# Another order for a mixture of experts' products on one core, and a routing whose splits are all VectorE's

## The chip, the cores and the metric

One of the eight cores of a Trainium2 chip runs the whole program: two layers of a first block (a state space mixer, an attention that picks its keys, two MLPs) and then a block with two attentions and 32 experts. The metric is the device time of one execution in microseconds. Five engines work side by side, each through its own list of instructions in order: TensorE (PE, with its weight loads PEld), VectorE (DVE), ScalarE (ACT), GpSimd (POOL) and SyncE (SP). SyncE starts nearly all loads from the chip's memory, GpSimd the gathers and the scattered additions; all of them are carried by the same 16 DMA engines.

## The reference, cut to what matters

The change touches the last block only. 512 tokens choose 4 of 32 experts each; an expert is three products of 1024 x 1024 with biases.

```python
logits = h @ router_w + router_b
top_logit, top_e = lax.top_k(logits, 4)
top_w = softmax(top_logit)
# for each expert e and the tokens xe that chose it
gate = minimum(xe @ w_gate[e] + b_gate[e], 7.0)
up = clip(xe @ w_up[e] + b_up[e], -7.0, 7.0)
act = (up + 1) * (gate * sigmoid(1.702 * gate))
y[tokens] += top_w * (act @ w_down[e] + b_down[e])
```

Everything is in float32. The 32 experts' weights are 403 MB, and each is read once.

## The kernel before

**Ranks and sizes.** The routing counts each expert's tokens and sorts the experts: rank 0 is expert 0 by fixed choice, then the ranks go down in size. The program is written for capacities by rank. Rank 1 has two tiles of 128 tokens, ranks 2 and 3 (`HEAVY` is 1 to 3) a tile of 128 and one of 64, ranks 0 and 4 to 10 one tile of 128; these eleven are called large here, the last eight middle. Ranks 11 to 21 (`LIGHT`) have 64 tokens, ranks 22 to 31 (`TINY`) 32. What does not fit goes through a loop at the end (`overflow`).

**Products.** An expert has three units: gate (0), up (1) and down (2), each with four loads of 1 MB (`fetch`, L1429) into eight buffers (`raw`). For a large expert ScalarE rounds each half of a load to a high part `wh` (L1772), VectorE forms the low part `wl` (L1774), and three matmuls of 128x512 are made of each (high by high, high by low, low by high: L170 to L172), over two halves of the columns and eight blocks of rows: 48 matmuls a tile, and 2 for the bias (L1832), which comes from a tile that holds the biases as high and low parts (`bias`). A tile of 64 tokens holds high and low parts side by side and needs 32 and 2 (L1826, L1827). A load's buffer is free when the low part is made. There are five buffers each for `wh` and `wl`, so splits run at most two and a half loads ahead of the matmuls. For small experts (light and tiny) TensorE takes the weights as they are, in full float32 (L1804), with 2 or 4 column groups side by side; such a buffer is free when the matmuls of the load are done. After the matmuls VectorE and ScalarE form gate and up, and GpSimd adds the weighted rows of down to the output (L1890). The rows of an expert's tokens are gathered by GpSimd some units earlier (L1713) and transposed by TensorE (L1738, L1727).

**What sets the order.** `units` writes out the list of the 96 units, and `run` goes through it; every engine's list follows from that. Before, the large experts come as 0, 4, 1, 5, 2, 6, 3, 7, 8, 9, 10, and two units of small experts stand ahead of each large unit: behind a heavy expert's name in the list tiny ones are drawn, else light ones. The small units form a `lane` in which a small expert's down comes one unit after the next one's gate. A unit issues its loads as it goes, so SyncE's queue has the loads in this order, and one of them waits until a buffer of the eight is free; large units ask for their first two loads (`ahead`) while the small unit before is at work.

**Routing.** `route` runs between the last logits and the first product. It loads the biases to raw tiles, which lie in three of the five `wh` buffers (L1528), and forms their high parts (L1530) and low parts (L1533) as they come. `first` finds the tokens of expert 0, gathers its rows (`gather`, L1713) and transposes and splits them (`tiles`, L1738, L165, L166), so that its product can start before the ranks are known. The rest sorts the experts (`perm`, L1559), transposes the sums (L1570), applies the order (L1575, L1576) and counts the ranks within each expert (L1587, L1588, `place` L1597). For the first two loads of expert 0's gate, GpSimd forms the low parts in VectorE's place (L1774, the `early` case).

## Time and profile before

| | |
|---|---|
| median of three runs | 2980.98 us (2974.2 to 2983.88) |
| the profiled execution | 2984.59 us, of which the span from first to last instruction 2982.8 us |
| TensorE busy, granted clock over the span | 2677.6 us (90%), 0.946 |
| VectorE, ScalarE, GpSimd busy | 1770.5, 1191.8, 245.2 us |
| bytes over the DMA engines | 595.95 MB, 200 GB/s over the span |
| first and last matmul of the experts | 1826.3 and 2966.3 us |

Times in the rows are from the start of the span. A row of the windows view has its bounds, its length, then for each engine the busy time and, in brackets, the instructions, then the granted clock of TensorE as a share of full, the mean busy share of the 16 DMA engines (which reaches 1.02 in the records) and the rate in GB/s. A row of a timeline has start, duration from the first start to the last end of the merged instructions, engine, line, operation, output and inputs, shapes, the number of instructions (x), and in square brackets the idle time of the engine before it with what ended that. Matmuls overlap, so one that takes 0.39 us can follow another 0.23 us after it; of a small expert's full float32 matmul (L1804) the records hold two instructions.

### The profile page before, as it was taken

What the parts mean: (1) busy time and instruction counts of PE and PEld (TensorE: products, weight loads), DVE (VectorE), ACT (ScalarE), POOL (GpSimd) and SP (SyncE); (2) the same over time, 40 slices, a digit from 0 to 9 for tenths busy, and PEclk for the clock granted to TensorE, in tenths of its full rate; (3) what the DMA queues carried; (4) which work ended last, traced back from release to release, by engine and by line L of the source; (5) the groups of instructions that cost most, each with busy time, mean ns of one, the idle gap of its engine ahead of it and who ended that gap; (6) DMA issues with size and microseconds to landing.
All of it is one profiled execution on the core that took longest, in us unless ns stands there. A gap on an engine that the chain in (4) does not pass through costs nothing. (4 is left out here: it accounts for less than half of the span.)

```text
span 2982.8 us, 38289 instructions
## 1 busy us (share of the span) xinstructions
PE 2677.6 (90%) x14182; PEld 1996.0 (67%) x14182; DVE 1770.5 (59%) x3419; ACT 1191.8 (40%) x2208; POOL 245.2 (8%) x229
## 2 busy tenths in 40 slices
PE   5599999987999999899998997999989989988986
PEld 3488777886778888788888775556455455444553
DVE  6967565578874444589777558444444444444443
ACT  5353232454863333366655434332233232333232
POOL 3000000142000000200000002110110110110010
PEclk9799999998999999999999997999989999999997
DMA  3024454321023333211122555998999998999997
GB/s 116 15 99 176 150 197 156 94 60 54 29 93 127 96 96 99 93 50 41 53 60 72 181 198 203 385 361 358 349 353 363 342 357 353 350 359 376 381 406 295
DMA packets 193999, 595.95 MB, mean 200 GB/s; under 512 B 34960, under 2 KB 106056, under 8 KB 141320
## 3 DMA queue, kind: packets, MB, share of 16 engines
q1 hardware_dynamic: 179744, 564.33, 50.8%
q0 software_dynamic: 8752, 28.58, 3.4%
q8 instruction: 113, 1.85, 0.2%
q10 hardware_dynamic: 5312, 0.54, 0.1%
q14 instruction: 78, 0.64, 0.1%
HBM read 574.49 MB, written 21.53 MB: 200 GB/s over the span
## 5 line engine op out<-in xcount | busy, mean ns | idle before, releaser
L1804 PE MATMUL lac<-raw,xtf 128*32 128x256 f32 (+1 forms) x2976 | 378.6, 461 | 6.4 <-DMA raw<-in_w_down_dram 3.8
L152 DVE TENSOR_TENSOR wl<-wr,wh 128x1024 fp32r<-128x1024 f32 (+2 forms) x222 | 262.3, 1187 | 177.6 <-ACT wh L150 173.8
L150 ACT CAST wh<-wr 128x1024 fp32r<-128x1024 f32 (+2 forms) x228 | 228.8, 1008 | 295.4 <-PE acc L172 162.0
L1774 DVE TENSOR_TENSOR wl<-raw,wh 128x1024 fp32r<-128x1024 f32 x260 | 303.7, 1219 | 36.3 <-ACT wh L1772 35.2
L171 PE MATMUL wide<-wl,xth 128*128 128x512 f32 x576 | 259.8, 451 | 30.8 <-DVE wl L1774 30.6
L170 PE MATMUL wide<-wh,xth 128*128 128x512 f32 x576 | 256.1, 446 | 33.7 <-ACT wh L1772 32.4
L1772 ACT CAST wh<-raw 128x1024 fp32r<-128x1024 f32 x264 | 260.8, 1045 | 62.5 <-PE wide L172 37.0
L1804 PEld LDWEIGHTS lac<-raw,xtf 128*32 128x32 f32 (+1 forms) x2976 | 126.3, 119 | 193.8 <-issue 155.2
L170 PE MATMUL mm<-wh,xh 128*128 128x384 f32 (+2 forms) x664 | 230.1, 346 | 27.0 <-ACT gate L1264 12.8
L172 PE MATMUL wide<-wh,xtl 128*128 128x512 f32 x576 | 250.2, 434 | 0.0
L171 PE MATMUL mm<-wl,xh 128*128 128x384 f32 (+2 forms) x664 | 222.7, 335 | 3.1 <-DVE wl L152 2.9
L172 PE MATMUL mm<-wh,xl 128*128 128x384 f32 (+2 forms) x664 | 222.5, 335 | 1.2 <-DVE xl L166 1.2
L171 PE MATMUL acc<-wl,ffh 128*128 128x512 f32 x512 | 199.3, 389 | 0.7 <-DVE wl L152 0.7
L172 PE MATMUL acc<-wh,ffl 128*128 128x512 f32 x512 | 199.4, 390 | 0.0
L170 PE MATMUL acc<-wh,ffh 128*128 128x512 f32 x512 | 198.6, 390 | 0.0
L171 PEld LDWEIGHTS wide<-wl,xth 128*128 128x128 f32 x576 | 122.2, 212 | 99.4 <-DVE wl L1774 56.2
L170 PEld LDWEIGHTS wide<-wh,xth 128*128 128x128 f32 x576 | 121.3, 211 | 88.9 <-ACT wh L1772 46.6
L170 PEld LDWEIGHTS mm<-wh,xh 128*128 128x128 f32 x664 | 129.0, 194 | 44.1 <-ACT gate L1264 17.1
L172 PEld LDWEIGHTS wide<-wh,xtl 128*128 128x128 f32 x576 | 122.2, 212 | 34.7 <-issue 11.4
L171 PEld LDWEIGHTS mm<-wl,xh 128*128 128x128 f32 x664 | 129.0, 194 | 9.8 <-DVE wl L152 5.3
L172 PEld LDWEIGHTS mm<-wh,xl 128*128 128x128 f32 x664 | 129.2, 195 | 7.0 <-DVE xl L166 1.9
L1890 POOL DMA_INDIRECT out_dram<-xy,si x35 | 65.4, 1867 | 662.1 <-DVE xy L1889 482.2
(641 smaller groups left out, 5417.7 us busy)
## 6 DMA issues: line engine op xcount, KB each, us to landing
raw<-in_w_gate_dram SPq DMA_DIRECT2D x128, 1024.0 KB, 8.5
raw<-in_w_up_dram SPq DMA_DIRECT2D x128, 1024.0 KB, 11.4
raw<-in_w_down_dram SPq DMA_DIRECT2D x128, 1024.0 KB, 7.3
wr<-in_mlp_w_dram SPq DMA_DIRECT2D x128, 512.0 KB, 3.7
adaraw<-in_w_ada_dram SPq DMA_DIRECT2D x12, 2048.0 KB, 7.5
wr<-in_w_in_dram SPq DMA_DIRECT2D x16, 512.0 KB, 3.9
wr<-in_att_w_out_dram SPq DMA_DIRECT2D x12, 512.0 KB, 3.9
wr<-in_w_in_dram SPq DMA_DIRECT2D x48, 128.0 KB, 2.4
```

What stands on the lines that cost most here:

```text
L150: nc.scalar.copy(hi, raw)
L152: (eng or nc.vector).tensor_tensor(lo, raw, hi.bitcast(F32), op=OP.subtract)
L170: mmul(ps, ah, bh, start=first, stop=False)
L171: mmul(ps, ah, bl, start=False, stop=False)
L172: mmul(ps, al, bh, start=False, stop=last)
L1772: S.copy(wh, raw[:, j])
L1774: (G_ if early and t == 0 and c < 2 else V).tensor_tensor(wl, raw[:, j], wh.bitcast(F32), op=OP.subtract)
L1804: T.matmul(ps[m * g:m * g + m], x, raw[:, j, N * g:N * g + N], start=False, stop=c == 3 and j == 1)
L1890: G_.indirect_dma_start(out=out_rows, out_offset=bass.IndirectOffsetOnAxis(ap=si[:rows], axis=0), in_=y, in_offset=None, bounds_check=511, ...
```

## The change

Three things are altered. In `units`, the table `many` names for every large expert how many units of small experts follow each of its three units: 1 for ranks 0, 4, 6, 7 and 9, 2 for ranks 5, 8 and 10, 4 for rank 1, 3 for ranks 2 and 3; behind heavy experts these are tiny ones, behind the others light ones. The sequence of large experts and the `lane` stay. In `expert`, VectorE forms all low parts. In `route`, only the loads of the raw biases stay at the head; their high and low parts are formed at the end of the function, and so is expert 0's transposed tile, which `first` had made.

```diff
 def units():
-    small = []
-    for r in big[1:]:
-        for _ in range(2):
-            n = next(tiny) if r in HEAVY else next(light, None)
-            small.append(next(tiny) if n is None else n)
+    light, tiny = iter(LIGHT), iter(TINY)
+    many = [(0, 1), (4, 1), (1, 4), (5, 2), (2, 3), (6, 1), (3, 3), (7, 1), (8, 2), (9, 1), (10, 2)]
+    small = [next(tiny if r in HEAVY else light) for r, n in many for _ in range(n)]
     lane = [(small[0], 0), (small[0], 1)]
     for p, r in zip(small, small[1:]):
         lane += [(r, 0), (p, 2), (r, 1)]
...
-    order = [(0, 0), (0, 1), next(lane), (0, 2)]
-    for u in [(r, t) for r in big[1:] for t in range(3)]:
-        order += [next(lane), next(lane), u]
-    return order + list(lane)
+    lane = iter(lane + [(small[-1], 2)])
+    order = []
+    for r, n in many:
+        for t in range(3):
+            order += [(r, t)] + [next(lane) for _ in range(n)]
+    order[1:3] = order[2:0:-1]
+    return order
@@ route
+        raws = []
         for n in ("b_gate_2", "b_up_2", "b_down_2"):
-            raw = self.wp.tile([P, D], F32, name="bw", tag="wh")[:, :512]
+            raws.append(self.wp.tile([P, D], F32, name="bw", tag="wh")[:, :512])
             for i in range(4):
...
-            x = bp.tile([P, 512], F32R, name=n)
-            S.copy(x, raw)
-            for i in (1, 3):
-                s = slice(NE * i, NE * i + NE)
-                V.tensor_tensor(x[s], raw[s], x[s].bitcast(F32), op=OP.subtract)
-            self.bias.append(x)
@@ route, at its end
         V.tensor_copy(self.cnt, o)
+        self.xt0 = self.tiles(self.x0)
+        for n, raw in zip(("b_gate_2", "b_up_2", "b_down_2"), raws):
+            x = bp.tile([P, 512], F32R, name=n)
+            S.copy(x, raw)
...
@@ first
-        x0 = self.gather(gi)
+        self.x0 = self.gather(gi)
...
-        self.xt0 = self.tiles(x0)
@@ expert
-                    (G_ if early and t == 0 and c < 2 else V).tensor_tensor(wl, raw[:, j], wh.bitcast(F32), op=OP.subtract)
+                    V.tensor_tensor(wl, raw[:, j], wh.bitcast(F32), op=OP.subtract)
```

The engines' lists are not in the order of the code alone; a scheduler lays them out. VectorE's list in the routing, before, from the operands of expert 0's gather (`gi`) to the third block's sums (`sw` is the sums, `sv` what comes of expert 0's table):

```order
L1641 TENSOR_SCALAR gi_16459<-tr 128x1
L1550 TENSOR_TENSOR one<-one,w_16423 128x128
L1649 CAST ax_16441<-w_16464 128x4
L1550 TENSOR_TENSOR one<-one,w_16423 128x128
L1650 TENSOR_TENSOR ax_16441<-w_16464,ax_16441 128x4
L1551 TENSOR_REDUCE sw<-one 128x32
L1533 TENSOR_TENSOR b_up_16410<-bw,b_up_16410 32x512 x2
L1666 COPY sv_16474<-tr 128x4
L1551 TENSOR_REDUCE sw<-one 128x32
```

and after:

```order
L1543 SCALAR_TENSOR_TENSOR kc<-mm,c_keyc 128x1
L1769 TENSOR_TENSOR wl<-raw,wh 128x1024
L1637 TENSOR_SCALAR gi_16447<-tr 128x1
L1644 TENSOR_REDUCE w_16452<-w_16451 128x4
L1538 TENSOR_TENSOR one<-one,w_16411 128x128
L1645 CAST ax_16429<-w_16452 128x4
L1538 TENSOR_TENSOR one<-one,w_16411 128x128
L1646 TENSOR_TENSOR ax_16429<-w_16452,ax_16429 128x4
L1539 TENSOR_REDUCE sw<-one 128x32 x2
L1661 COPY sv_16462<-tr 128x4
```

The two subtractions of b_up's low part stand between the sums before and have left; one split (`wl<-raw`) now stands ahead of `gi`.

TensorE's list in the routing, before, from expert 0's two tables to the counts of the ranks (`xy` is expert 0's gathered tile, `sw` the sums):

```order
L1639 MATMUL tr<-ax_16441,oh 128x4 x4
L1653 MATMUL tr<-ax_16441,oh 128x4 x4
L1738 MATMUL tr<-c_ident,xy 128x128 x8
L1570 MATMUL tr<-c_ident,sw 64x128 x4
L1575 MATMUL out<-two,rxt 128x64 x4
L1576 MATMUL out<-perm,c_tokp_72 128x32
L1588 LDWEIGHTS before
```

and after:

```order
L1635 MATMUL tr<-ax_16429,oh 128x4 x4
L1649 MATMUL tr<-ax_16429,oh 128x4 x4
L1558 MATMUL tr<-c_ident,sw 64x128 x4
L1563 MATMUL out<-two,rxt 128x64 x4
L1564 MATMUL out<-perm,c_tokp_72 128x32
L1733 MATMUL tr<-c_ident,xy 128x128 x8
L1576 LDWEIGHTS before
```

The tile's eight transpositions stood ahead of the sums' transposition and its products; they now stand behind.

TensorE's list at a heavy expert, before, from the last matmuls of rank 1's gate product to the first of its up product (`lac` is a small expert's product, 64x512 for light and 32x256 for tiny ones):

```order
L1804 MATMUL lac<-raw,xtf 32x256 x8
L170 MATMUL wide<-wh,xth 128x512
L171 MATMUL wide<-wl,xth 128x512
L172 MATMUL wide<-wh,xtl 128x512
L1727 MATMUL tr<-c_ident,gl 128x128 x2
L1796 MATMUL lac<-b_down_16419,pick 128x256 x2
L1700 MATMUL tr<-aux,ohs 128x4 x4
L1727 MATMUL tr<-c_ident,xg 128x128 x4
L1804 MATMUL lac<-raw,xtf 32x256 x8
L1700 MATMUL tr<-aux,ohs 128x4 x4
L1796 MATMUL lac<-b_up_16410,pick 128x256 x2
L170 MATMUL wide<-wh,xth 128x512 x2
```

and after, all that stands between the two:

```order
L1799 MATMUL lac<-raw,xtf 64x512 x16
L1791 MATMUL lac<-b_up_16583,pick 128x256 x2
L1799 MATMUL lac<-raw,xtf 32x256 x16
L1791 MATMUL lac<-b_gate_16579,pick 128x256
L1799 MATMUL lac<-raw,xtf 32x256 x8
L1791 MATMUL lac<-b_gate_16579,pick 128x256
L1799 MATMUL lac<-raw,xtf 32x256 x8
L1791 MATMUL lac<-b_down_16587,pick 128x256 x2
L1722 MATMUL tr<-c_ident,gl 128x128 x2
L1695 MATMUL tr<-aux,ohs 128x4 x4
L1722 MATMUL tr<-c_ident,xg 128x128 x2
L1799 MATMUL lac<-raw,xtf 32x256 x24
```

Before, eight matmuls of a tiny down product lie between the two large ones, and the rest of the small units among the large product's; after, a whole light down product, a whole tiny up product and 24 of the 32 matmuls of a tiny gate product stand between them.

## Rows read from the trace of the kernel before

**Rows 1.** Stretch of the experts' products: length, engines' busy us, clock, DMA share, GB/s

```profile
1826.30:2966.30 1140.00, 1032.34 (x5553) 612.01 (x5553) 547.55 (x811) 358.75 (x489) 101.51 (x68) 0.93 0.93 361
```

**Rows 2.** The same view: the stage in eleven pieces, mostly between large gate products' ends

```profile
1826.30:1906.10 79.80, 79.80 (x344) 51.65 (x344) 51.72 (x91) 34.27 (x39) 7.67 (x5) 0.97 0.87 346
1906.10:2021.40 115.30, 104.32 (x567) 63.35 (x570) 54.31 (x91) 34.33 (x48) 13.82 (x9) 0.93 0.94 362
2021.40:2136.80 115.40, 108.88 (x601) 66.50 (x598) 54.38 (x80) 34.04 (x49) 10.96 (x8) 0.97 0.90 339
2136.80:2245.10 108.30, 97.90 (x534) 58.18 (x534) 48.28 (x71) 31.70 (x42) 9.21 (x6) 0.92 0.95 369
2245.10:2362.30 117.20, 105.79 (x570) 63.97 (x569) 58.83 (x88) 37.90 (x56) 10.62 (x8) 0.93 0.89 340
2362.30:2470.50 108.20, 97.26 (x534) 58.15 (x537) 47.97 (x71) 31.60 (x42) 9.51 (x6) 0.92 0.95 369
2470.50:2587.30 116.80, 105.93 (x567) 63.90 (x567) 58.11 (x87) 37.93 (x55) 9.58 (x7) 0.93 0.88 340
2587.30:2695.40 108.10, 98.75 (x395) 50.74 (x396) 49.13 (x70) 31.48 (x40) 9.17 (x6) 0.94 0.96 370
2695.40:2799.00 103.60, 94.01 (x425) 49.37 (x426) 48.76 (x71) 31.53 (x42) 9.17 (x6) 0.95 0.94 361
2799.00:2887.90 88.90, 77.61 (x546) 47.59 (x550) 44.00 (x56) 31.85 (x45) 7.60 (x4) 0.94 1.01 407
2887.90:2966.30 78.40, 62.09 (x503) 38.61 (x502) 32.06 (x38) 22.14 (x31) 4.20 (x3) 0.84 0.95 389
```

**Rows 3.** Timeline of TensorE (start us, us, engine, line, operation, tiles, shapes)

```profile
1902.74 0.39 PE L171 MATMUL wide<-wl,xth 128*128 128x512 f32 x1
1902.97 0.39 PE L172 MATMUL wide<-wh,xtl 128*128 128x512 f32 x1
...
1906.24 3.65 PE L1804 MATMUL lac<-raw,xtf 128*64 128x512 f32 x16
...
2904.39 3.72 PE L1804 MATMUL lac<-raw,xtf 128*32 128x256 f32 x64
...
2910.47 0.80 PE L170 MATMUL wide<-wh,xth 128*128 128x512 f32 x1 [1.32 <-ACT wh L1772]
...
2914.03 0.63 PE L170 MATMUL wide<-wh,xth 128*128 128x512 f32 x1
2914.46 0.63 PE L171 MATMUL wide<-wl,xth 128*128 128x512 f32 x1
```

**Rows 4.** Timeline of VectorE in the routing

```profile
1799.87 0.68 DVE L1533 TENSOR_TENSOR b_gate<-bw,b_gate 32x512 fp32r<-32x512 f32 x1
...
1804.70 8.55 DVE L1533 TENSOR_TENSOR b_up<-bw,b_up 32x512 fp32r<-32x512 f32 x2
...
1815.23 1.61 DVE L1559 TENSOR_SCALAR perm<-c_iota,kc 128x32 f32<-128x32 f32 x1
...
1820.56 1.22 DVE L1774 TENSOR_TENSOR wl<-raw,wh 128x1024 fp32r<-128x1024 f32 x1
...
1824.33 0.19 DVE L1578 TENSOR_SCALAR permf<-out 128x32 f32<-128x32 f32 x1 [2.55 <-PE out L1576]
```

**Rows 5.** Timeline of GpSimd in the routing

```profile
1804.69 1.03 POOL L1713 DMA_INDIRECT xy<-hx,gi  x1 [6.72 <-DVE sw L1551]
...
1805.75 6.94 POOL L1774 TENSOR_TENSOR wl<-raw,wh 128x1024 fp32r<-128x1024 f32 x3
...
1814.46 2.34 POOL L1774 TENSOR_TENSOR wl<-raw,wh 128x1024 fp32r<-128x1024 f32 x1 [1.77 <-ACT wh L1772]
```

**Rows 6.** Timeline of TensorE in the routing

```profile
1809.15 1.10 PE L1738 MATMUL tr<-c_ident,xy 128*128 128x128 f32 x4 [3.62 <-DMA xy<-hx,gi]
...
1820.04 1.06 PE L1570 MATMUL tr<-c_ident,sw 128*64 128x128 f32 x4 [5.41 <-DVE xtl L166]
...
1826.27 0.77 PE L170 MATMUL wide<-wh,xth 128*128 128x512 f32 x1 [0.57 <-DVE cnt L1610]
```

More of the change, by code (lines that the diff above doesn't have):

```diff
@@ L1367, in units @@
 def units():
-    mids, light, tiny = list(range(HEAVY[-1] + 1, LIGHT[0])), iter(LIGHT), iter(TINY)
-    big = [0]
-    for h in HEAVY:
-        big += [mids.pop(0), h]
-    big += mids
-    small = []
-    for r in big[1:]:
-        for _ in range(2):
-            n = next(tiny) if r in HEAVY else next(light, None)
-            small.append(next(tiny) if n is None else n)
-    small += list(light) + list(tiny)
+    light, tiny = iter(LIGHT), iter(TINY)
+    many = [(0, 1), (4, 1), (1, 4), (5, 2), (2, 3), (6, 1), (3, 3), (7, 1), (8, 2), (9, 1), (10, 2)]
+    small = [next(tiny if r in HEAVY else light) for r, n in many for _ in range(n)]
     lane = [(small[0], 0), (small[0], 1)]
@@ L1383, in units @@
         lane += [(r, 0), (p, 2), (r, 1)]
-    lane.append((small[-1], 2))
-    lane[-3:] = [lane[-2], lane[-3], lane[-1]]
-    lane = iter(lane)
-    order = [(0, 0), (0, 1), next(lane), (0, 2)]
-    for u in [(r, t) for r in big[1:] for t in range(3)]:
-        order += [next(lane), next(lane), u]
-    return order + list(lane)
+    lane = iter(lane + [(small[-1], 2)])
[5 more added lines that the diff above has]
+    return order
 class Moe:
@@ L1524, in route @@
         self.bias = []
+        raws = []
         for n in ("b_gate_2", "b_up_2", "b_down_2"):
[L1526 removed]
+            raws.append(self.wp.tile([P, D], F32, name="bw", tag="wh")[:, :512])
             for i in range(4):
[L1528 to L1534 removed]
+                nc.gpsimd.dma_start(raws[-1][NE * i:NE * i + NE], a[n][0][:, i // 2 * 512:i // 2 * 512 + 512])
         m8, one, sw, selb, onesb, iota = self.m8, self.one, self.sw0, self.selb, self.onesb, self.iota
@@ L1610, in route @@
         V.tensor_copy(self.cnt, o)
+        self.xt0 = self.tiles(self.x0)
+        for n, raw in zip(("b_gate_2", "b_up_2", "b_down_2"), raws):
+            x = bp.tile([P, 512], F32R, name=n)
+            S.copy(x, raw)
+            for i in (1, 3):
+                s = slice(NE * i, NE * i + NE)
+                V.tensor_tensor(x[s], raw[s], x[s].bitcast(F32), op=OP.subtract)
+            self.bias.append(x)
     def pools(self):
```

1 line of the change is left out of this document (removed).

## The prediction

> **What bounds the kernel now.** I read the stretches first, then the timelines of the engines where the change works. [rows 1] is the stage of the experts' products, 1140.0 us at a DMA share of 0.93 and a granted clock of 0.93; ahead of it lies the routing, in which TensorE mostly waits. In the stage neither engine is full, so the question is who waits for whom and where. [rows 2] cuts it into eleven pieces, each but the first and last between the ends of the gate products of two neighbouring large experts (nine products a piece). Let me call (1 - share) x length the DMA time that is lost. It is 10.4, 6.9, 11.5, 5.4, 12.9, 5.4, 14.0, 4.3, 6.2, 0 and 3.9 us: 80.9 in all. The three pieces of 0.88 to 0.90 are those with two products of a heavy expert (ranks 1, 2, 3); the piece of 1.01 has only tiny experts behind its large ones and loses nothing. So the transfers take 1140 - 81 = 1059 us, and for the 94 products that are still to be loaded (two are prefetched) that is 11.27 us a product. TensorE's own need: matmuls of a large product start 0.228 us apart at the full clock [rows 3], so a product of one tile (50 matmuls) needs 11.4 us, rank 1 (100) 22.8, ranks 2 and 3 (84) 19.2; a light product needs 7.3 us (twice the 3.65 of half a product), a tiny one 4.0 (3.72 and its biases) [rows 3]. A large product is thus at or above the loads' pace, a small one below it, and eight buffers of 1 MB carry a surplus of two products at most.
>
> The routing is a chain with one odd spot. VectorE's two subtractions for b_up take 8.55 us together, though one of the same on b_gate took 0.68 [rows 4]. Beside them GpSimd runs three splits from 1805.75 on, 6.94 us, until 1812.69 [rows 5]; VectorE gets free right behind that. The `perm` of the ranks takes 1.61 us beside the fourth Pool split, 1814.46 to 1816.80; `permf`, of the same size, takes 0.19 [rows 4, 5]. Everything of the ranks waits behind: the first transposition of the sums at 1820.04, the first large matmul at 1826.27 [rows 6].
>
> **The change, part by part.** *Pool's splits go to VectorE, the biases' parts behind the ranks.* The chain from 1804.70 on loses 8.55 us. It gains 1.22 (one split, the price of [rows 4]), which now stands ahead of `gi`, whose gather feeds expert 0's tile: the gather goes out at 1805.9 in place of 1804.69 [rows 5], and its transpositions, 1809.15 before [rows 6], come at 1810.4. `perm` then ends at 1816.84 - 8.55 + 1.22 - 1.4 = 1808.1. In the old program the ranks' transposition had waited 5.41 us for `xtl`, expert 0's tile, by 1820.04, because both go through the same two PSUM banks [rows 6]; the new order puts the ranks' transpositions and their products ahead of the tile's. From 1820.04 to `permf` at 1824.33 it was 4.3 us, so `permf` comes at about 1812.4, the tile's eight transpositions take 2.2 us (1.10 for four [rows 6]), the ranks' counts follow at 1814.7, `cnt` and `place` as before 1.8 us later, with half of b_down's part (0.7) in between: 1817.2 for the first large matmul, against 1826.27. The other splits wait on VectorE behind b_down, the second row block at 1819.5; the first six matmuls at half clock (0.43 us each, [rows 3]) cover that nearly. Gain 9 us. Bounds: 4 us, if three of the extra splits (3 x 1.22) and the 1.22 in the gather's path all stand in the way; 12 us, if the ranks' counts do not wait for the tile's transpositions. I take 9, since each step has its row.
>
> The Trainium skill (SBUF — State Buffer, section Who interferes with whom) says that a VectorE instruction with two SBUF inputs and a GpSimd instruction that reads SBUF exclude each other, the later one blocking until the one that holds the port is through. By the letter, one Pool split (6.94 / 3 = 2.3 us) would be the price and the gain nearer to 4 us. The trace has VectorE blocked through all three splits, so I keep 9; with 4 it would be 2966, inside the forecast's own range.
>
> What the cover was: GpSimd's splits freed the first two load buffers at 1810.4 and 1816.8; now they come free about 9 us later, at 1819.5 and 1822. These loads are expert 0's down weights, used two products later only, so it costs nothing; the buffers behind them are freed by the products themselves and move up by the 9 us. GpSimd's queue has only the next gathers behind the splits, and these wait for the ranks anyway. The overflow's small sums move behind the first product on VectorE: nothing waits for them.
>
> *The order of the experts.* No matmul, load or evacuation is added or removed; every product keeps its price. What changes is which loads stand behind which large product. The load of TensorE by a group (a large product and what follows it), against 11.27 us a product:
> before: rank 1 with two tiny 30.8 of 33.8 = 0.91; ranks 2, 3 with two tiny 27.2 = 0.80, with one light and one tiny 30.5 = 0.90, with two light 33.8 = 1.0; a middle one with two light 26.0 = 0.77; with two tiny, at the end, 19.4 = 0.57.
> after: a middle one with one light (12 groups beside expert 0's three) 18.7 of 22.5 = 0.83; with two light (9 groups) 0.77; rank 1 with four tiny 38.8 of 56.4 = 0.69; ranks 2 and 3 with three (6 groups) 31.2 of 45.1 = 0.69.
> From [rows 2] the loss of each load: the two pieces with six groups of 0.77 lose 10.5, 1.75 each or 5.2% of 33.8. The six pieces with heavy experts (9 heavy products, 9 middle ones) lose 56.1; less 9 x 1.75 leaves 40.4, 4.5 a heavy product or 13% at a load of about 0.9. At 0.57 nothing is lost. On that line 0.83 loses 9%, 2.0 us a group, and 0.69 loses 3%. After: 12 x 2.0 = 24; 9 x 1.75 = 16; heavy 3% of (3 x 56.4 + 6 x 45.1) = 14; the first piece 10 and the end 4 as before. That is 68 in place of 81: 13 us gained. Bounds: 40 gained (no loss at heavy ones and none added), and a loss of 36 (the second rival). It's a small gain by a table that looks much better balanced, because the light experts, which cost nearly twice a tiny one, now all stand behind the middle ones.
>
> Sum: 2984.6 (the profiled execution) - 9 - 13 = 2962.6. The runs' median, 2981.0, lies 3.6 lower; part of that is scatter (2974.2 to 2983.9), and I forecast 2961.
>
> **The rivals.**
> *Order neutral, 0.22.* Middle groups lose as much as heavy ones save: then only the 9 us are left, 2972 to 2976. For it: the two sums of loss above differ by a sixth only, and a piece as a whole (nine products) shows a loss that rises between 0.77 and 0.81 of load more steeply than my line.
> *One light product can't carry a middle one, slower, 0.11.* With one light behind it, a middle product has 22.5 - 18.7 = 3.8 us for everything else (transpositions, tables, waits for splits, half clock). Above that TensorE sets the pace there, while behind the heavy ones the loads set it, and eight buffers don't join the two. The piece from 2587.3 has 108.1 us for 78 us of products: 10 us per large one, if none of it is waiting for loads. Then: first six products 68, twelve groups of 28.7 = 344, nine of 36 = 324, 39 products behind and with the heavy ones at 11.27 = 440, together 1176 for 1140: +36 - 9, so 3011. Against it: the first piece, where the loads lay ready, has 79.8 us for 67.5 of products, 3.1 us per large one, just below the point. At 2910.47 a large product waits 1.32 us and then runs at 0.43 us a matmul [rows 3], half clock, 3.2 us in all over 16 matmuls.
> The Trainium skill (TensorE: Matmul & The Clock Gate, section HAM oscillation) has it that bursts between waits for transfers start throttled each time. By that, 3.2 us would come on top of the 3.1, 6.3 per large one: 2.5 us over the point in twelve groups, 30 us, and a time of 2991; of the 0.11 I put 0.03 on this form. The clock of 0.84 in the last piece [rows 2] agrees; that of 0.97 in the first, where TensorE was never starved, is why I don't charge it to middle groups.
> *Large gain, 0.13.* The heavy ones' 40 us go wholly and middle groups lose only their 5.2%: 44 us lost in place of 81, 2981 - 46 + 3 = 2938.
> *No gain in the routing, 0.07.* Expert 0's first product waits for the splits on VectorE or for its loads; the order alone gives 2968 to 2972.
>
> **How the numbers follow.** Forecast 0.47, at 2950 to 2970. A difference under 0.3% (8.9 us: below 2972.0 or above 2989.9) can't be told from none. Faster: 0.93 of the forecast, a third of the neutral case, the large gain, half of the last rival: 0.68. Slower: nearly all of the second rival, 0.11. The rest, 0.21, is the same. The range leaves out half of the slower rival above and the ends of the large gain below: 2930 to 2990.
>
> **What would show it.** Routing: no VectorE instruction of more than 1.3 us between 1800 and 1817, transpositions of the sums ahead of the tile's, the first large matmul at 1816 to 1819. Order: the pieces with heavy experts at a DMA share of 0.96 or more, the middle pieces with one light at 0.90 to 0.93, the stage some 1127 us long. Wrong, if the heavy pieces keep 0.88 to 0.90, if a middle group with one light takes more than 25 us, or if the last loads land later behind the end of TensorE's work than now.

## The result

| | median | runs |
|---|---|---|
| before | 2981.77 us | 4 (2974.2 to 2983.88) |
| changed | 2913.26 us | 4 (2912.07 to 2914.09) |

The ratio is 0.9775 [0.9759, 0.979]: 68 us faster. The forecast of 2961 and its range, 2930 to 2990, had the sign right and the size three times too small.

The profiled execution has a span of 2911.1 us (2982.8 before). Of these 71.7 us, 55.3 lie in the stage of the products. The last bias load goes out at 1792.32 in place of 1797.48, 5.2 us earlier, and it lies ahead of anything that the change touches; the profiled executions further down have it between 1787.5 and 1796.1, so that of before began its routing late, and I take these 5.2 us for scatter. The routing gives another 12, and the end behind the last matmul is 0.7 us longer than it was.

The stage in stretches, most again from the end of one large gate product to the end of another (us, length, busy time of the five engines, granted clock, DMA share, GB/s; the last row is the whole stage):

```profile
1809.20:1892.80 83.60, 81.72 (x353) 52.36 (x353) 58.76 (x99) 35.76 (x43) 7.31 (x5) 0.95 0.90 356
...
1970.50:2128.40 157.90, 139.38 (x1057) 85.73 (x1060) 63.69 (x112) 39.62 (x63) 17.72 (x13) 0.94 1.00 398
...
2237.40:2367.80 130.40, 117.00 (x809) 72.73 (x812) 61.63 (x100) 39.67 (x61) 18.13 (x10) 0.91 0.98 387
...
2438.10:2565.80 127.70, 114.54 (x807) 71.07 (x807) 60.91 (x99) 39.48 (x60) 17.20 (x9) 0.93 1.00 403
2565.80:2635.20 69.40, 64.88 (x324) 38.87 (x324) 44.35 (x64) 30.07 (x39) 8.54 (x5) 1.00 0.99 390
2635.20:2740.40 105.20, 96.02 (x387) 48.98 (x388) 47.74 (x63) 31.00 (x39) 8.23 (x5) 0.95 0.98 382
2740.40:2811.40 71.00, 67.37 (x283) 38.09 (x283) 41.85 (x50) 29.29 (x36) 6.72 (x3) 1.00 0.95 363
2811.40:2893.90 82.50, 75.66 (x311) 34.81 (x310) 33.48 (x38) 20.48 (x25) 5.43 (x3) 0.98 0.84 333
1809.20:2893.90 1084.70, 999.20 (x5553) 593.57 (x5553) 552.38 (x818) 359.98 (x494) 113.58 (x68) 0.96 0.96 382
```

Read against [rows 1, 2]: the stage went from 1140.0 to 1084.7 us, TensorE's busy time in it from 1032 to 999, the clock from 0.93 to 0.96, the transfers from 361 to 382 GB/s. The pieces with two products of a heavy expert (157.9 us with 15 products, 130.4 and 127.7 with 12) now take 10.5 to 10.9 us a product at a share of 0.98 to 1.00, where they took 12.8 to 13.0. The piece with one light product behind each of three middle ones (71.0 us for six, from 2740.40) takes 11.8; one like it, in which one of the three is tiny (69.4, from 2565.80), takes 11.6. The piece with two light ones (105.2 for nine, from 2635.20) takes 11.7, 3 us less in all than the same nine products before (108.1, from 2587.30 in [rows 2]).

The kinds of the small products need a correction. The lane puts a small expert's down product behind the next one's gate, so what stands behind a large product is shifted against what was drawn for it. Of the 30 small products behind heavy experts 24 are tiny and six light; of the twelve that stand singly behind middle ones four are tiny.

The routing, TensorE and then VectorE:

```profile
1806.24 1.98 PE L1733 MATMUL tr<-c_ident,xy 128*128 128x128 f32 x8
...
1809.16 0.77 PE L170 MATMUL wide<-wh,xth 128*128 128x512 f32 x1 [0.57 <-ACT pick L1755]
```

```profile
1802.30 0.23 DVE L1547 TENSOR_SCALAR perm<-c_iota,kc 128x32 f32<-128x32 f32 x1
...
1802.62 0.68 DVE L1605 TENSOR_TENSOR b_up<-bw,b_up 32x512 fp32r<-32x512 f32 x1
...
1806.35 0.19 DVE L1566 TENSOR_SCALAR permf<-out 128x32 f32<-128x32 f32 x1 [1.15 <-PE out L1564]
```

`perm` takes 0.23 us (1.61 in [rows 4]), a part of b_up 0.68 (8.55 for two), and the first large matmul follows the last bias load's issue by 16.8 us, where it was 28.8 (1826.27 in [rows 6] less 1797.48).

Part of this is given back. The first piece of the stage takes 83.6 us, and 79.2 with the same order and the old routing (`order_alone`, experiment 1). VectorE, and then TensorE, in the changed kernel:

```profile
1811.33 6.90 DVE L1769 TENSOR_TENSOR wl<-raw,wh 128x1024 fp32r<-128x1024 f32 x6
...
1819.81 0.69 DVE L1692 TENSOR_TENSOR ohs<-slot,place 128x512 fp32r<-128x512 f32 x1
```

```profile
1830.30 0.78 PE L1722 MATMUL tr<-c_ident,xg 128*128 128x128 f32 x4 [1.76 <-DMA xg<-hx,gi]
```

Seven splits (six of them in this row) now stand ahead of the tables of the next experts (`ohs`), which begin 10.7 us behind the first large matmul; in `order_alone` it is 0.5. The gather of the next rows goes out 14.8 us behind that matmul, 11.8 in `order_alone`, and TensorE waits 1.76 us for it. The matmuls behind that wait start 0.43 us apart at first, at half clock, where they were 0.23 apart. How much of the 4.4 us this makes was not tested.

### The profile page after: what moved, and what is told of

Same layout as the page of the kernel before. It is cut to its first block, busy times and chain, and to the rows that moved or that the text cites. A ratio compares the mean times of both kernels' runs of the same rounds, so it can differ in the third digit from the quotient of the medians.

```text
span 2911.1 us, 38304 instructions
## 1 busy us (share of the span) xinstructions
PE 2642.2 (91%) x14182; PEld 1975.6 (68%) x14182; DVE 1765.1 (61%) x3423; ACT 1191.3 (41%) x2208; POOL 248.4 (9%) x225
## 5 line engine op out<-in xcount | busy, mean ns | idle before, releaser
L171 PE MATMUL wide<-wl,xth 128*128 128x512 f32 x576 | 252.4, 438 | 30.1 <-DVE wl L1769 29.8
L170 PE MATMUL wide<-wh,xth 128*128 128x512 f32 x576 | 245.0, 427 | 18.8 <-ACT wh L1767 18.1
L172 PE MATMUL wide<-wh,xtl 128*128 128x512 f32 x576 | 239.6, 416 | 0.0
L171 PEld LDWEIGHTS wide<-wl,xth 128*128 128x128 f32 x576 | 115.8, 201 | 101.4 <-DVE wl L1769 54.5
L170 PEld LDWEIGHTS mm<-wh,xh 128*128 128x128 f32 x664 | 128.5, 194 | 43.7 <-ACT gate L1264 16.8
L1885 POOL DMA_INDIRECT out_dram<-xy,si x35 | 75.7, 2163 | 609.9 <-DVE xy L1884 407.5
```

What stands on the lines that cost most here:

```text
L170: mmul(ps, ah, bh, start=first, stop=False)
L171: mmul(ps, ah, bl, start=False, stop=False)
L172: mmul(ps, al, bh, start=False, stop=last)
L1885: G_.indirect_dma_start(out=out_rows, out_offset=bass.IndirectOffsetOnAxis(ap=si[:rows], axis=0), in_=y, in_offset=None, bounds_check=511, ...
```

## The experiments

**1. Order and routing apart.** `order_alone` is the kernel before with the new `units`; `routing_alone` the changed kernel with the old one.

```diff
 def units():
-    for u in [(r, t) for r in big[1:] for t in range(3)]:
-        order += [next(lane), next(lane), u]
+    for r, n in many:
+        for t in range(3):
+            order += [(r, t)] + [next(lane) for _ in range(n)]
```

> The kernel before with the new order of the experts only; the routing keeps GpSimd's splits and the early biases' parts. Theory A (the order is worth nearly all of it, and the routing adds to it independently): the stage of the products takes 1085 to 1092 us in place of 1140, the first large matmul stays 28 to 30 us behind the last bias load's issue (28.8 before), and the time is 2923 to 2933. Rival B (the shorter routing is what gives the stage its head start, the order alone is worth the 13 us that I forecast): a stage of 1120 to 1130 and a time of 2965 to 2972.

> The changed kernel with the old order of the experts; only the routing is changed. Theory A: the first large matmul 16 to 18 us behind the last bias load's issue (16.8 in the changed kernel, 28.8 before), the stage 1135 to 1142 as before, the time 2967 to 2973, that is 9 to 15 less. Rival B: the stage shortens as well, to 1110 or less, and the time is under 2950.

Measured: `order_alone` 2922.95 us against 2979.32 for the kernel before on the same chip, 0.9826 [0.9809, 0.9843]; `routing_alone` 2969.33, 0.9965 [0.9954, 0.9976]. So 56 and 10 us, and together they make the 66 to 68 of the change. The order alone gives its stage without any help of the routing (the first piece and the whole stage of `order_alone`):

```profile
1821.40:1900.60 79.20, 79.17 (x346) 51.46 (x346) 51.84 (x91) 34.24 (x39) 7.68 (x5) 0.96 0.86 340
...
1821.40:2903.90 1082.50, 996.75 (x5553) 591.43 (x5553) 545.95 (x811) 358.62 (x492) 114.75 (x68) 0.96 0.96 380
```

Rival B is out. My 13 us for the order was the error.

**2. The routing's two halves.** Both have the new order. `biases_alone` keeps GpSimd's splits, `splits_alone` keeps the biases' parts and expert 0's tile in their old places.

```diff
 # biases_alone, against the changed kernel
-                    V.tensor_tensor(wl, raw[:, j], wh.bitcast(F32), op=OP.subtract)
+                    (G_ if early and t == 0 and c < 2 else V).tensor_tensor(wl, raw[:, j], wh.bitcast(F32), op=OP.subtract)
 # splits_alone, against order_alone
-                    (G_ if early and t == 0 and c < 2 else V).tensor_tensor(wl, raw[:, j], wh.bitcast(F32), op=OP.subtract)
+                    V.tensor_tensor(wl, raw[:, j], wh.bitcast(F32), op=OP.subtract)
```

> The changed kernel with the first four splits on GpSimd again; biases' parts stay behind the ranks. Read: time from the last bias load's issue to the first large matmul, 28.8 before and 16.8 in the changed kernel. Theory A (any VectorE instruction beside a GpSimd split is held up, so the stall moves to another instruction): 22 to 27 us, with one VectorE instruction of over 3 us among the ranks' ones beside GpSimd's splits. Rival (the biases' place was what cost): 16 to 19 us and no such instruction.

> The kernel before with the new order and with the first four splits on VectorE; the biases' parts and expert 0's tile stay where they were, ahead of the ranks. Read as in the run before. Theory A: 18 to 21 us (the 8.55 us stall is gone, 2 x 0.7 us of biases' parts and the tile's split stay ahead of the ranks). Rival (the place of biases and tile was what cost): 24 us or more.

Measured, from the last bias load's issue to the first large matmul: 24.5 us in `biases_alone`, 24.7 in `splits_alone`; 29.0 in `order_alone`, 16.8 with both. The halves give 4.4 and 4.3 us alone, both together 12.1. In `biases_alone` the stall only moved. VectorE, then GpSimd:

```profile
1800.96 7.20 DVE L1538 TENSOR_TENSOR one<-one,w 128x128 f32<-128x128 f32 x1
```

```profile
1801.06 6.93 POOL L1769 TENSOR_TENSOR wl<-raw,wh 128x1024 fp32r<-128x1024 f32 x3
```

A VectorE instruction that took 0.28 us in the changed kernel took 7.20 beside three splits. In `splits_alone` the stall is gone, but I had expected 18 to 21 us. TensorE there:

```profile
1808.43 1.95 PE L1731 MATMUL tr<-c_ident,xy 128*128 128x128 f32 x8 [3.54 <-DMA xy<-hx,gi]
...
1811.13 1.06 PE L1563 MATMUL tr<-c_ident,sw 128*64 128x128 f32 x4 [0.75 <-DVE xtl L166]
...
1819.29 0.77 PE L170 MATMUL wide<-wh,xth 128*128 128x512 f32 x1 [1.42 <-DVE cnt L1603]
```

The ranks' transpositions (1811.13) still stand behind the gathered tile's, and the biases' parts ahead of that delay the gather too (1803.85, 9.3 us behind the last bias load; 7.6 in the changed kernel). So the stall and the place were two covers of one wait: either alone leaves the other.

**3. Is it the kind or the number of the small products?** `two_each` has two behind each large one as before, but draws strictly tiny ones for heavy experts; `kinds` has the change's numbers, with the draws of light and tiny ones exchanged. By the lane's shift, six of the 18 small products behind heavy experts are still light in `two_each`, where before nine were; in `kinds` 24 of 30 are light, where the change has six.

```diff
 # two_each
-    many = [(0, 1), (4, 1), (1, 4), (5, 2), (2, 3), (6, 1), (3, 3), (7, 1), (8, 2), (9, 1), (10, 2)]
+    many = [(0, 1)] + [(r, 2) for r in (4, 1, 5, 2, 6, 3, 7, 8, 9, 10)]
-    small = [next(tiny if r in HEAVY else light) for r, n in many for _ in range(n)]
+    small = [next(tiny if r in HEAVY or r > 8 else light) for r, n in many for _ in range(n)]
 # kinds
-    small = [next(tiny if r in HEAVY else light) for r, n in many for _ in range(n)]
+    small = [next(light if r in HEAVY else tiny, None) or next(light) for r, n in many for _ in range(n)]
```

> The changed kernel with another order: two small products behind every large one as before, but strictly tiny ones behind ranks 1 to 3 and light ones behind middle ones (before, the last product of each heavy expert had one or two light ones behind it); the last four tiny experts stand behind ranks 9 and 10. Theory L (what decides is TensorE's need of a whole group against its loads): heavy groups at 27.2 and 30.8 us for three loads of 10.7 us are still near 0.9, so about half of the 56 us stays won: 2935 to 2950. Theory K (only the kind matters: no light product behind a heavy one): nearly all stays won, 2925 or less. Theory N (only the number matters: three or four behind a heavy one): nearly all is lost, 2958 to 2970.

> The changed kernel with its numbers of small products behind each large one kept, but light experts behind the heavy ones and tiny ones behind the middle ones. Theory L: heavy groups at 41 to 52 us of TensorE for four or five loads (43 and 53 us) are at 0.96 or more and lose as much as before the change, the pieces with heavy experts at 350 GB/s or less: 2962 to 2985. Theory K the same. Theory N: no change, 2910 to 2920.

Measured: `two_each` 2975.21, 0.9995 [0.9986, 1.0004], all of the order's gain gone; `kinds` 2918.86, 0.9798 [0.9781, 0.9816], nearly all kept. Only theory N came near both times (5 us above its range with the first, inside it with the second), the one for which I had no mechanism. `kinds` refuses theory K. `two_each` hardly changed the kinds, so it shows that two behind each is dear and says little of kinds.

The line of my prediction gets no support from `kinds` either: its heavy groups need 38 to 52 us of TensorE for the loads of four or five products, 0.88 to 0.97 of them at 10.7 us a product, and yet the time is that of the change to 6 us. But the pieces did not stay as they were. Its two other heavy pieces beside that of rank 3 (experiment 8):

```profile
1965.90:2130.80 164.90, 159.66 (x798) 84.18 (x798) 66.89 (x112) 38.63 (x57) 16.80 (x13) 0.99 0.96 374
...
2239.20:2380.30 141.10, 131.67 (x647) 70.56 (x644) 63.94 (x100) 38.84 (x57) 14.85 (x10) 0.95 0.90 342
```

The three take 438.6 us, 22.6 more than in the changed kernel, with TensorE busy for 417 of them; the others, which gave light products for tiny ones, take 16 less together. So the equal time of `kinds` is in part a balance of the two.

**4. The pace of the loads.** `loads_alone` leaves out two of the three matmuls of each triple in the large products, and one of the two for a tile of 64 tokens; all loads and splits stay.

```diff
-   kk.mm3(o, x[0], x[1], wh[:, hs], wl[:, hs], first, last)
+   T.matmul(o, x[0], wh[:, hs], start=first, stop=last)
```

> The changed kernel with two of the three matmuls of each triple of the large products left out (the parts with the weights' low halves and the tile's low halves; the second tile of ranks 2 and 3 loses its low half too), all loads, splits and small products as they are: the pace of the loads when TensorE hardly holds them up. Theory F (the DMA share hides slow transfers; a product's loads take 10.7 us at best, as in the changed kernel's heavy pieces): 395 GB/s or more over the stage, 1015 to 1040 us long. Theory on record (11.27 us a product, from one minus the DMA share): 1070 us or more, hardly shorter than the changed kernel's 1084.7.

```profile
1807.10:2832.90 1025.80, 791.36 (x4305) 372.99 (x4305) 554.21 (x818) 365.29 (x494) 99.60 (x68) 0.87 1.00 403
2200.00:2500.00 300.00, 223.84 (x1552) 114.23 (x1550) 155.19 (x242) 104.33 (x153) 27.71 (x21) 0.85 1.01 410
```

The stage takes 1026 us when TensorE hardly holds the loads up, 10.9 us a product with start and end, and 410 GB/s in its middle. My floor of 11.27 us was too high: before, 361 GB/s stood at a share of 0.93, so the transfers that were under way were slower than these (361/0.93 = 388, 410/1.01 = 406). By 410 GB/s the stage before lost, as an estimate, 1140 x (1 - 361/410) = 136 us, not 81.

**5. Needs that match.** If two engines with equal needs and a short store between them were what costs, more TensorE work in the heavy pieces would bring the loss back. `tiny_more`, and `tiny_double` with 7 in place of 3:

```diff
-                    for g in range(G):
+                    for g in range(G + (G if G == 4 and 2 * c + j < 3 else 0)):
+                        g %= G
```

> The changed kernel with three of the eight steps of each tiny product issued twice (its sum is not the reference's): 1.4 us more of TensorE for each of the 30 tiny products, 12.5 us in a piece with nine of them. There TensorE's need goes from 114 to 117 us to 127 to 130, the loads' is 127 to 128. Theory M (two engines whose needs match within a few per cent, with a store of two products between them, lose about 10 us a piece of nine products; where one of them leads clearly, next to nothing): the three heavy pieces become 8 to 15 us longer each, the GB/s there fall from 387 to 403 to 365 or less, and the time rises by 25 to 45, to 2938 to 2958. Theory S (a piece takes the longer of the two needs, whatever the distance): each heavy piece stays within 4 us of what it was, 2913 to 2925.

> The same with seven of eight steps twice: 3.25 us more a tiny product, 29 us in a piece with nine, so that TensorE needs 144 to 146 us there for loads of 128. Theory M: the heavy pieces are 147 to 152 us long, that is, less than 6 us over TensorE's need, at a granted clock near 1.00; the time is 2975 to 2995. Theory S: 145 to 147 us, 2970 to 2980. If a piece exceeds TensorE's need by 10 us here too, then matching needs are not what costs.

Measured: 2917.11 and 2960.42 (one run each). The three heavy pieces of `tiny_more` that were 157.9, 130.4 and 127.7 us, and then the second of them in `tiny_double`:

```profile
1967.40:2133.30 165.90, 150.46 (x1297) 92.90 (x1298) 63.72 (x112) 39.50 (x63) 16.86 (x13) 0.96 0.97 384
...
2241.90:2371.60 129.70, 121.62 (x976) 75.63 (x980) 61.83 (x100) 39.47 (x61) 14.39 (x10) 0.95 0.97 381
2444.50:2571.00 126.50, 118.39 (x974) 73.35 (x978) 61.08 (x99) 39.27 (x60) 13.46 (x9) 0.97 1.00 398
```

```profile
2257.60:2395.40 137.80, 131.38 (x1201) 80.59 (x1204) 61.73 (x100) 39.26 (x61) 14.11 (x10) 0.98 0.93 362
```

These two runs don't decide between the theories, because the needs that I had planned weren't reached. There are seven tiny products in each of the two shorter pieces, not nine, and the granted clock rose with the added work (0.91 to 0.95 and 0.93 to 0.97), so TensorE's busy time rose by 4 to 5 us only, and not by 12.5. These pieces got no longer, but the first, with ten tiny products and 11 us more of TensorE's busy time, got 8.0 us longer, as theory M had it. The total of `tiny_more`, 2917, is theory S's. In `tiny_double` the two pieces exceed TensorE's busy time by 6 us, about what theory M allows. What settles theory M is experiment 7, where the loss goes while every need stays.

**6. Fewer pairs, and a smaller store.** `heavy4` moves the pairs behind ranks 5 and 8 to the heavy experts, `ring6` takes two load buffers away, `tiny_end1` has a tiny expert last.

```diff
 # heavy4
-    many = [(0, 1), (4, 1), (1, 4), (5, 2), (2, 3), (6, 1), (3, 3), (7, 1), (8, 2), (9, 1), (10, 2)]
+    many = [(0, 1), (4, 1), (1, 4), (5, 1), (2, 4), (6, 1), (3, 4), (7, 1), (8, 1), (9, 1), (10, 2)]
-    small = [next(tiny if r in HEAVY else light) for r, n in many for _ in range(n)]
+    small = [next(tiny if r in HEAVY else light, None) or next(light) for r, n in many for _ in range(n)]
 # ring6
-RAWS = 8
+RAWS = 6
 # tiny_end1
+    small = [next(tiny if c == "t" else light) for c in "ll" "tttt" "ll" "ttt" "l" "tlt" "l" "ll" "l" "lt"]
```

> The changed kernel with four small products behind each heavy one and one behind each middle one but the last: (4, 1), (1, 4), (5, 1), (2, 4), (6, 1), (3, 4), (7, 1), (8, 1), (9, 1), (10, 2); rank 3 gets two tiny and two light ones for each of its products. Theory M: the pieces of middle experts with two light products (100 us of TensorE for loads of 96, 105 to 109 us long) give way to ones with one (70 us for six products) and to heavy pieces that the loads lead clearly: 5 to 15 us less, 2898 to 2908. Theory S: TensorE leads in all middle pieces and the loads in all heavy ones, the sum of the longer needs rises: 2915 to 2930.

> The changed kernel with six load buffers of 1 MB in place of eight (and so six prefetched loads). Theory M and the store: with one and a half products in store the needs are coupled more tightly; the pieces with two light products and those with one get longer by 5 to 10 us each, the time rises by 30 to 80. If the store is not what couples them, the time rises by the two prefetched loads alone, 5 us or less.

> The changed kernel with the last small expert a tiny one, in exchange for one light expert whose three products now stand behind rank 3's. In the changed kernel TensorE works for some 18 us behind the landing of the last loads. Theory L: the group of a heavy product with two tiny and one light (34.5 us of TensorE for 42.7 us of loads, 0.81) loses nothing, and the end is shorter by a tiny in place of a light product or two: 2905 to 2910. Theory K: each of the three groups loses 4 us or more, 2915 to 2925.

Measured: `heavy4` 2896.00, 0.9733 [0.972, 0.9746], 17 us less than the change; `ring6` 2948.64 (one run), 35 us more, so the store matters; `tiny_end1` 2909.74, 0.9779 [0.9766, 0.9793], no difference from the change that can be told. `heavy4` came nearest to theory M, 2 us under its range. What it shares with the other results is simpler: the number of groups with exactly two small products ahead of a large one. It is 30 before, in `routing_alone` and `two_each`, 9 in the change, `kinds` and `tiny_end1`, 3 in `heavy4`.

**7. When a large product's first loads are asked for.** A small unit looks two units ahead, and has the first two loads of a large product there fetched and split. With exactly two small products, it is the first one behind a large product that does this, before the second one's loads are asked for. (The section on the kernel before has these loads asked for while the small unit right before is at work; that is so only where one small product stands between two large ones.) The next runs move only that: the three called near as shown, `new_far` with `i + 4` and an end at the first large product.

```diff
-                    for q, tq in todo[i + 1:i + 3]:
+                    for q, tq in todo[i + 1:i + 2]:
```

> The changed kernel with the old order (as routing_alone, 2969), and the look-ahead of a small product cut from two products to one: the first two chunks of a large product are asked for and split in the middle of the small product right in front of it, not of the one before that. Theory W (with two small products between large ones these chunks are loaded while the large product before still holds the split buffers; they lie in two of eight load buffers, 24 us from issue to release before and 16 us behind the change for the heavy ones): most of the 56 us comes back without any change of order, 2915 to 2940. Rival E (the time that the evacuation and transpositions of a large expert need between its products decides, and two small products are too few for it): the splits come later still, 2969 to 2990.

> The changed kernel with the look-ahead lengthened from two products to three, up to the next large one: with three or four small products behind a heavy one, the next large product's first chunks are asked for one small product earlier; groups with one or two stay as they are. Theory W: the pieces with heavy experts lose transfers again, GB/s of 360 or less in place of 387 to 403, and the time rises by 15 to 35: 2928 to 2948. Rival E: nothing changes or it gains, 2908 to 2918.

> The changed kernel with the look-ahead of one product. Theory W: groups with two light products (nine of them, 105 to 109 us for nine products) gain 2 to 4 us each, the heavy ones little: 2890 to 2908. Rival E: large products start later, 2913 to 2930.

> The order of heavy4 (2896) with the look-ahead of one product. There only the last three groups have two small products, so theory W leaves little: 2888 to 2898. Rival E: 2896 to 2910.

Measured: `old_near` 2883.47, 0.9674 [0.9654, 0.9695]: the order of before with one number changed is 86 us faster than the same without it, and faster than the changed kernel. `new_near` 2884.25, 0.968 [0.9661, 0.97]. `heavy4_near` 2897.42, 0.9732 [0.9709, 0.9754], the same as `heavy4`, where three pairs were left to gain from. `new_far` 2916.43, 0.9796 [0.9774, 0.9819], no change, against theory W. With the later request the order has nothing left to give: the old one takes 2883.47 us and the new one 2884.25, where with the early request they were 56 us apart. The stage and some of its pieces in `routing_alone` and then in `old_near`. In each, the piece from 2351.50 or 2308.00 has rank 6's up and down, rank 3's gate and six small products, the one from 2571.70 or 2512.50 has six light products, the one from 2782.80 or 2700.30 has five tiny ones and a light one; that of `old_near` from 1997.60 has two products of rank 1:

```profile
1811.50:2949.00 1137.50, 1027.06 (x5553) 608.10 (x5553) 553.86 (x818) 359.89 (x491) 102.06 (x68) 0.94 0.94 364
2351.50:2456.70 105.20, 94.07 (x533) 55.84 (x537) 47.96 (x71) 31.61 (x42) 9.53 (x6) 0.95 0.95 370
2571.70:2679.30 107.60, 98.52 (x394) 50.73 (x396) 49.12 (x70) 31.47 (x40) 9.19 (x6) 0.94 0.95 370
2782.80:2871.70 88.90, 77.62 (x546) 47.63 (x550) 43.95 (x56) 31.86 (x45) 7.61 (x4) 0.94 1.01 412
```

```profile
1807.20:2867.30 1060.10, 978.95 (x5553) 587.65 (x5553) 556.55 (x818) 363.09 (x491) 103.73 (x67) 0.97 0.98 391
1997.60:2106.10 108.50, 105.17 (x603) 67.69 (x601) 54.20 (x80) 34.29 (x49) 11.96 (x8) 0.98 0.93 362
2308.00:2405.70 97.70, 89.60 (x532) 54.41 (x535) 48.42 (x71) 32.03 (x42) 9.47 (x6) 0.98 1.02 413
2512.50:2608.60 96.10, 92.36 (x394) 46.72 (x394) 49.17 (x70) 31.58 (x40) 10.53 (x6) 1.00 1.01 410
2700.30:2793.60 93.30, 77.89 (x547) 46.96 (x547) 44.42 (x56) 32.00 (x45) 6.41 (x4) 0.93 1.02 416
```

77.4 us in 30 pairs are 2.6 us a pair on average: 1.0 of TensorE's idle time (110.4 to 81.2 us) and 1.6 of its busy time (1027 to 979, at a clock of 0.94 and 0.97). The pieces differ. The three with two products of a heavy expert got 7.0 to 10.9 us shorter, the two with five or six light products 11.5 and 11.8, and the one with tiny products, where the loads lead (1.01), 4.4 longer.

TensorE's list shows how. Rank 6's up product in `routing_alone`, then in `old_near`:

```profile
2356.70 0.50 PE L170 MATMUL wide<-wh,xth 128*128 128x512 f32 x1
...
2361.05 1.94 PE L1806 MATMUL lac<-raw,xtf 128*64 128x512 f32 x8
...
2367.28 5.37 PE L1806 MATMUL lac<-raw,xtf 128*64 128x512 f32 x24
...
2375.48 0.49 PE L170 MATMUL wide<-wh,xth 128*128 128x512 f32 x1 [0.56 <-ACT wh L1774]
2376.74 0.50 PE L171 MATMUL wide<-wl,xth 128*128 128x512 f32 x1 [0.77 <-DVE wl L1776]
...
2382.32 0.39 PE L172 MATMUL wide<-wh,xtl 128*128 128x512 f32 x1
```

```profile
2320.70 0.50 PE L170 MATMUL wide<-wh,xth 128*128 128x512 f32 x1
...
2325.06 1.94 PE L1806 MATMUL lac<-raw,xtf 128*64 128x512 f32 x8
...
2335.67 0.39 PE L172 MATMUL wide<-wh,xtl 128*128 128x512 f32 x1
```

With the early request the product falls apart: its first half runs from 2356.70, then come the small product's matmuls (lac), and the second half, whose loads were asked for behind those of the second small product, waits for its splits from 2375 on. It is 26 us from end to end; with the later request 15.4. The waits for splits in the whole stage, again `routing_alone` and then `old_near` (us in total, times, longest):

```profile
PE wide L171 <- DVE wl L1776: 32.1, 46, 2.0
PE wide L170 <- ACT wh L1774: 31.9, 32, 3.0
```

```profile
PE wide L170 <- ACT wh L1774: 18.7, 14, 4.3
PE wide L171 <- DVE wl L1776: 16.8, 37, 0.8
```

The early loads also lie longer in the store: from issue to the end of their second subtraction 24 us for both sorts of large product in `routing_alone`, 17.4 (middle) and 18.8 (heavy) in `old_near` (means over 38 and 18 loads). Theory W made the split buffers the reason for that; no run here has more of them, so it stays open whether it is these buffers or the order in SyncE's queue that makes the early request dear.

**8. Why `new_far` lost nothing.** There the requests were early behind heavy experts, where the loads lead: in the changed kernel TensorE is busy 114.5 of 127.7 us there. Its groups of three and four have an early request already, made by the last small product but one. Without it (`new_near`) the three heavy pieces are 6.7 us shorter together, 0.7 a group; the three pieces with pairs are 24.2 us shorter. In `kinds`, with light products there, TensorE is busy 126 of 133 us in the piece of rank 3. `kinds_far` makes the edit of `new_far` on `kinds`. `best` puts the findings together: the later request, tiny experts at the start and at the end where TensorE sets the pace, light ones behind heavy experts.

```diff
 # best, against new_near
+    small = [next(tiny if c == "t" else light) for c in "t" "t" "tltl" "ll" "ttl" "l" "ttt" "l" "ll" "l" "lt"]
```

> The order of kinds (light experts behind heavy ones, 2919; in the heavy pieces TensorE is busy 126 to 160 us of 133 to 165) with the look-ahead lengthened from two products to three, up to the next large one. In new_far the same lengthening cost nothing, where the loads led. Theory W2 (an early request costs where TensorE has no slack, since its waits and half clock then lengthen the stage): the nine heavy groups lose 2.6 to 4 us each, 2940 to 2955. Rival X (only a pair of small products has the loss, whatever the slack): no change, 2912 to 2925.

> The numbers of small products of the changed kernel with the look-ahead of one product (new_near, 2884) and another choice of kinds: tiny experts behind ranks 0 and 4, where TensorE sets the pace after the start (83 and 78 us for 6.7 and 6.4 products), two light ones among rank 1's four, one among rank 2's, and a tiny expert last. Theory (pieces led by TensorE get shorter by 3.3 us for each light product exchanged for a tiny one, pieces led by the loads have slack for it): 10 to 15 us less than new_near, 2868 to 2878. Rival (slack in the heavy pieces is needed against stalls): 2880 to 2892.

Measured: `kinds_far` 2941.97, 0.9873 [0.9855, 0.9892], 23 us more than `kinds`, 2.6 for each of its nine heavy groups: theory W2. The piece of rank 3 in `kinds` and then in `kinds_far`:

```profile
2459.60:2592.20 132.60, 125.91 (x644) 67.26 (x643) 63.21 (x99) 39.05 (x58) 13.97 (x9) 1.00 0.93 365
```

```profile
2472.50:2617.10 144.60, 133.66 (x645) 70.36 (x644) 63.65 (x99) 39.23 (x58) 12.07 (x9) 0.95 0.89 342
```

12 us longer, 8 of them TensorE's busy time at a lower clock. So no pair is needed, only an early request where TensorE has no slack. `best` took 2870.54 us, 0.9637 [0.9621, 0.9654], the fastest of all: 14 less than `new_near` and 43 less than the changed kernel, with 397 GB/s over its stage.

```profile
1808.50:2852.00 1043.50, 972.48 (x5553) 581.05 (x5553) 555.89 (x818) 362.70 (x491) 106.77 (x68) 0.98 0.99 397
```

## Why the prediction was wrong, step by step

- **Routing, 9 us: right in mechanism, a little small.** 12.0 us by the traces, 10 by `routing_alone`'s runs; 12 was my upper bound. The term that I had left out is the first piece of the stage, 4.4 us longer than with the old routing. Less the 5.2 us that lie ahead of it, `permf` came 0.9 us earlier than I had worked out. The rest is that the tile's transpositions (1806.24) ran beside it and not behind it, so that the ranks' counts waited for little. No VectorE instruction over 1.3 us stands between 1800 and the first large matmul, as forecast, and the sums' transpositions stand ahead of the tile's.
- **The early splits as a mere cover: right for the load buffers only.** Nothing waited for these. But I had looked only at what GpSimd's queue holds behind the splits, and not at what VectorE's now holds behind them: the next experts' tables, for whose gather TensorE waits 1.76 us.
- **Order, 13 us: the failed step.** "The loss of each load": I took the DMA time lost in a piece as a function of TensorE's need in each group against its loads, and put heavy groups at 13% and middle ones with one light product on a line up to 9%. When a large product's first loads are asked for was no term of that sum. `old_near` shows that it is what decides: it has every load, need and group of `routing_alone`, and a stage 77.4 us shorter. The loss was 2.6 us a pair on average, from loads asked for and split one product too early. To groups with two light products I had given 1.75 us; the two pieces with nearly only such groups got 3.9 a group shorter, the heavy ones 2.9. The change took 21 of 30 pairs away, twelve for groups of one, where no request is that early, and nine for groups of three and four, where the loads lead. 21 x 2.6 = 55 us, where the stage lost 55.3; that this comes out so closely is luck, since the pieces differ. In [rows 2] the cause couldn't be seen, because every group was a pair but one: the pieces differed by kind only, and so kind seemed to explain what they lost. And a low share there is in part no loss: the piece of `old_near` from 1997.60 still has 0.93, with TensorE busy 105.2 of 108.5 us. That the order gained, as I had forecast, was right for another reason than mine, and so luck.
- **The groups after the change.** My table of loads had only tiny products behind heavy experts and only light ones behind middle ones. With the lane's shift the heavy groups stand at 0.69 to 0.77 and four of the twelve single ones at 0.68. By my own line these two nearly cancel, so this is not what made the sum wrong.
- **The floor of 11.27 us a product: wrong.** It came from one minus the DMA share. `loads_alone` moves 410 GB/s at a share of 1.01, and the heavy pieces now take 10.5 to 10.9. The "large gain" rival, counted from the same shares, stood at 2938, short of what came. The Trainium skill (Perfetto Trace Analysis, section Identifying the Most-Contended Engine) advises to judge DMA by HBM utilization and not by occupancy, which 16 engines make misleading; the 361 GB/s at 0.93 and 410 at 1.01 bear it out.
- **The signs that I had named.** Heavy pieces at 0.96 or more: yes (0.98 to 1.00). Middle pieces with one light product at 0.90 to 0.93: no, 0.95 to 1.00. A stage of 1127 us: no, 1084.7.
- **One light product can't carry a middle one: no.** Such a group takes 23.7 us (71.0 / 3), between the 18.7 that I had for TensorE and the bound of 25. At a clock of 1.00 it runs without the restarts at half clock that this rival charged.

## What to carry to other kernels

Before you explain slow stretches by the size of the work in them, write down what all of them have in common: here it was the moment at which a unit's first loads are asked for, and one number in the look-ahead was worth more (86 us) than the new order (56); with it, the new order gained nothing more. A request that is too early splits a long product in two and makes its second half wait; here that cost much where TensorE had no slack (`kinds_far`) and nothing that can be told where the loads led (`new_far`). Measure the pace of the loads by leaving out work, or by GB/s, not by the share of time in which the queues are busy.

## What was not expected of the hardware

A VectorE instruction with two inputs waited through three GpSimd splits in a row: 7.20 us for one that takes 0.28 alone, and 1.63 for a cast of 32 numbers beside the fourth split (`biases_alone`, at 1813.87). The Trainium skill (SBUF — State Buffer, section Who interferes with whom) has the later of the two block until the one that holds the port is through, which would be one split, 2.31 us; here it was all three, although the VectorE instruction's record starts 0.1 us ahead of theirs. And a DMA share of 0.93 to 0.95 went with 361 to 370 GB/s in most pieces (389 in the last of [rows 2]), one of 1.01 or 1.02 with 407 to 416: the share is a poor measure of the bytes.
